# Scan decays of a hybrid encoder layer: bias in the exponential, feature decays by broadcast, time steps held by token

## The chip, the cores and the metric

One core of one Trainium2 chip runs the kernel. The metric is device microseconds of one execution; the profile adds one execution with the start and end of every instruction. A core has five instruction queues that run at the same time and meet only at semaphores: PE (TensorE, with its weight loads shown as PEld), DVE (VectorE), ACT (ScalarE), POOL (GpSimd) and SP (SyncE, which here only starts transfers). Each queue runs strictly in its own order: an instruction that waits holds up everything behind it on the same engine.

## The reference

One layer, sequence length 512, width 1024. The part that the change touches is the Mamba-2 style scan, forward and backward, 32 heads in 4 groups of 8, state 128, chunks of 128 tokens:

```
dt    = softplus(dt_in + dt_bias)                        # per token and head, two directions
a_cum = cumsum(dt * (-exp(a_log)))                       # inside each chunk
decay[l, s] = exp(a_cum[l] - a_cum[s]) where s <= l      # 0 elsewhere
y_diag = (C B^T * decay) @ (x * dt)
states = B^T @ (to_end * dt * x);  carried over the 4 chunks
y_off  = exp(a_cum) * (C @ carried_state)
y = y_fwd + y_bwd + d_skip * x;  then a gated group RMSNorm and three projections
```

Around it: RMSNorm, one wide input projection, a five-tap depthwise convolution with SiLU, windowed attention, gated merge, cross-attention over 256 memory rows, a SwiGLU FFN and a final RMSNorm.

## The kernel before, in words

Activations lie feature-major (features on partitions, 512 tokens along the row). Every projection step takes one weight block of 128x1024 (a `raw` tile, two buffers, loaded by SP), splits it into a high part `whi` (ACT, L128) and a low part `wlo` (DVE, or POOL for nine blocks, L129), and runs 24 matmuls (L138 to L140) into one of three PSUM banks `mm`. A list of steps is written out by the program; a scheduler then fixes the order of the instructions on each engine, and inserts the waits.

The steps that matter here, in order of time:

- **The time-step step** (`dt_step`, L338 to L398) runs once, at about 55 us, right after the first projection. It computes the softplus of the 64 rows (32 heads, two directions) with a polynomial on DVE, in tiles of 64 partitions by 512 tokens (L348 to L362), turns the results to token-major on PE (L368), forms running sums by matmuls with triangles (L380, L387, L391), and writes the sums `adr` to DRAM (L383), so that they can be read back broadcast over partitions. It leaves `nb` (log dt minus the running sum), `wt` and `dec`, token-major.
- **The convolutions** (`conv`, L403): ACT starts the tile `cvu` from PSUM (L408), DVE adds four taps (L411), ACT takes a tanh (L413), DVE finishes (L414). For the feature blocks `xs` PE then transposes the result (L467); that is placed in PE's queue one projection later.
- **The scan of a group** (`group_scan`): POOL weighs the tokens (`xw`, L492), PE forms the states (L500), DVE carries them (L505, L507). For each head, `head(h)`: SP loads two broadcast rows of `adr` into `rt` (128 partitions by 2x512, three buffers; L516); ACT takes the exponential of one half of its partitions into `ear` (L528; two buffers, one for a pair of heads); POOL writes a large negative number where the decay is zero, in place, for both directions (L530); then for each of the four chunks ACT takes an exponential with the bias `nb` in the forward direction (L536) and DVE adds `nb` in the backward direction (L538), after which one ACT exponential covers all four (L539). `both(h)` adds the two directions on POOL (`mt`, L545, frees `rt`), `times(h)` multiplies by C B^T on DVE (L550), `inner` and `arrive` are PE's products, and `gather` adds everything up; its last sum, on POOL (L585), frees `ear`.

The steps of a group's scan are interleaved with the projections and convolutions of the next group.

## Time and profile before

| | |
|---|---|
| runs | 1328.16, 1330.67, 1332.9 us, median 1330.67 |
| the profiled execution | 1331.93 us, span of its instructions 1330.2 us |
| busy over the span | PE 95%, PEld 76%, DVE 61%, ACT 44%, POOL 24% |
| 56 to 530 us | PE busy 430.88 of 474 us, DVE 375.47, ACT 237.53, POOL 201.64 |
| 530 to 1330 us | PE busy 786.53 of 800 us, DVE 400.74, ACT 308.62, POOL 99.51 |

A busy PE is one with a matmul in flight. The first stretch of the last two rows holds the time-step step, the convolutions and the scan; the second everything behind them. PEclk in the windows is the mean of the clock granted to TensorE, 1.00 for 2.4 GHz; its other level is half of that, 1.2 GHz.

### The profile page before, as it was taken

The numbers are of one execution on the slowest core, as the hardware profiler recorded it, in microseconds if no ns is written. First come the engines' busy times: TensorE is split into PE (matmuls) and PEld (weight loads), VectorE is DVE, ScalarE is ACT, GpSimd is POOL, SyncE is SP. The second block draws the span as 40 slices with busy tenths as digits, with TensorE's granted clock in tenths as the row PEclk, the third lists the DMA queues.
The fourth block names the chain that finished last, engine by engine and source line by source line (L and its number), as shares of the span: only waits on it lengthen the run. The fifth ranks groups of instructions, "written<-read, shape, count | busy, mean of one in ns | idle before, by whom it ended". The sixth has DMA issues, their size and how long they took to land.

```text
span 1330.2 us, 16362 instructions
## 1 busy us (share of the span) xinstructions
PE 1259.6 (95%) x6084; PEld 1016.9 (76%) x6084; DVE 811.2 (61%) x1359; ACT 579.1 (44%) x1001; POOL 316.4 (24%) x259
## 2 busy tenths in 40 slices
PE   6879998998999899999999999999999999999996
PEld 5667777786777687887667888888888888888886
DVE  5896788789678876678875334665443334442323
ACT  6437366266346434167865223444332223332220
POOL 3344263244354452321000002001121111110001
PEclk9999999999999899999999999999999999999998
DMA  6425344243233332321103333411232332223331
GB/s 241 141 97 151 123 151 127 60 131 116 82 103 111 95 96 90 113 88 64 49 33 111 98 98 106 143 64 52 92 96 97 102 102 95 96 91 103 88 99 64
DMA packets 45440, 134.95 MB, mean 101 GB/s; under 512 B 5104, under 2 KB 8560, under 8 KB 45360
## 3 DMA queue, kind: packets, MB, share of 16 engines
q1 hardware_dynamic: 43072, 129.77, 30.8%
q10 hardware_dynamic: 1584, 2.03, 0.5%
q0 software_dynamic: 704, 2.10, 0.4%
q8 instruction: 48, 0.79, 0.2%
q14 instruction: 32, 0.26, 0.1%
HBM read 129.55 MB, written 4.33 MB: 101 GB/s over the span
## 4 chain that ended last, share of the span: by engine, by line
PE 62%; DVE 12%; issue 10%; POOL 7%; ACT 5%; DMA 2%; SPq 0%; DVEq 0%; POOLq 0%; ACTq 0%
PE mm L138 18%; PE mm L139 18%; PE mm L140 18%; DVE rt L538 2%; DVE cvu L411 2%; DVE wlo L129 2%; POOL vv L585 1%; PE sb L815 1%; POOL mt L545 1%; ACT whi L128 1%; PE sb L802 1%; DMA rt<-adr 1%; POOL rsw L714 1%; POOL rt L530 1%; PE sb L988 1%
## 5 line engine op out<-in xcount | busy, mean ns | idle before, releaser
L128 ACT CAST whi<-raw 128x1024 fp32r<-128x1024 f32 (+2 forms) x192 | 198.9, 1037 | 451.9 <-PE mm L139 388.2
L138 PE MATMUL mm<-hh,whi 128*128 128x512 f32 x968 | 384.9, 398 | 6.9 <-DVE cvu L411 5.4
L139 PE MATMUL mm<-hl,whi 128*128 128x512 f32 x968 | 380.4, 393 | 1.8 <-DVE hl L310 1.8
L140 PE MATMUL mm<-hh,wlo 128*128 128x512 f32 x968 | 380.6, 393 | 1.1 <-DVE wlo L129 1.0
L129 DVE TENSOR_TENSOR wlo<-raw,whi 128x1024 fp32r<-128x1024 f32 (+2 forms) x193 | 242.4, 1257 | 128.4 <-ACT whi L128 122.4
L138 PEld LDWEIGHTS mm<-hh,whi 128*128 128x128 f32 x968 | 183.8, 190 | 46.3 <-issue 8.2
L140 PEld LDWEIGHTS mm<-hh,wlo 128*128 128x128 f32 x968 | 183.4, 189 | 41.3 <-DVE wlo L129 2.9
L139 PEld LDWEIGHTS mm<-hl,whi 128*128 128x128 f32 x968 | 183.6, 190 | 39.3 <-DVE hl L310 3.0
L185 POOL TENSOR_TENSOR sq_acc<-sq_acc,sq 128x512 f32<-128x512 f32 x14 | 24.8, 1771 | 264.4 <-ACT sq L184 264.4
L1041 POOL TENSOR_TENSOR fa<-fa,row 128x512 f32<-128x512 f32 x22 | 39.1, 1776 | 192.4 <-ACT fa L1040 192.4
L411 DVE SCALAR_TENSOR_TENSOR cvu<-mm,hcw,cvu 128x510 f32<-128x510 f32 (+1 forms) x96 | 70.9, 739 | 4.3 <-ACT cvu L408 3.9
L138 PE MATMUL mm<-vh,whi 128*128 128x512 f32 (+1 forms) x192 | 72.5, 378 | 0.0
L138 PE MATMUL mm<-fh,whi 128*128 128x512 f32 (+1 forms) x198 | 72.4, 366 | 0.0
L139 PE MATMUL mm<-fl,whi 128*128 128x512 f32 (+1 forms) x198 | 72.4, 365 | 0.0
L140 PE MATMUL mm<-fh,wlo 128*128 128x512 f32 (+1 forms) x198 | 72.4, 365 | 0.0
L140 PE MATMUL mm<-vh,wlo 128*128 128x512 f32 (+1 forms) x192 | 70.0, 364 | 0.0
L139 PE MATMUL mm<-vl,whi 128*128 128x512 f32 (+1 forms) x192 | 69.5, 362 | 0.0
L538 DVE TENSOR_SCALAR rt<-rt,nb 128x128 f32<-128x128 f32 x128 | 52.4, 465 | 21.3 <-POOL rt L530 19.6
L545 POOL TENSOR_TENSOR mt<-rt 128x512 f32<-128x512 f32 x32 | 47.7, 1493 | 72.1 <-ACT rt L539 34.1
L1043 DVE TENSOR_TENSOR ft<-fa,mm 128x512 f32<-128x512 f32 x22 | 15.1, 688 | 73.2 <-PE mm L140 71.0
L528 ACT ACTIVATE ear<-rt 64x1024 f32<-64x1024 f32 x32 | 33.9, 1059 | 56.6 <-POOL vv L585 51.9
L139 PE MATMUL mm<-ol,whi 128*128 128x512 f32 x128 | 50.0, 391 | 0.0
(234 smaller groups left out, 2061.4 us busy)
## 6 DMA issues: line engine op xcount, KB each, us to landing
raw<-in_w_in SPq DMA_DIRECT2D x69, 512.0 KB, 3.5
raw<-in_w_fi SPq DMA_DIRECT2D x44, 512.0 KB, 3.5
rt<-adr SPq DMA_DIRECT2D x64, 256.0 KB, 4.4
raw<-in_w_bs SPq DMA_DIRECT2D x16, 512.0 KB, 3.4
raw<-in_w_fo SPq DMA_DIRECT2D x16, 512.0 KB, 3.5
raw<-in_w_xk SPq DMA_DIRECT2D x8, 512.0 KB, 3.8
raw<-in_w_ba SPq DMA_DIRECT2D x8, 512.0 KB, 3.5
raw<-in_w_mo SPq DMA_DIRECT2D x8, 512.0 KB, 3.5
```

The source lines that it names most:

```text
L128: nc.scalar.copy(hi[:, t], raw[:, t])
L129: (nc.gpsimd if i in LO_POOL else nc.vector).tensor_tensor(lo[:, t], raw[:, t], hi[:, t].bitcast(F32), op=ALU.subtract)
L138: nc.tensor.matmul(acc, wh, xh[:, k0 + k], start=first and k == 0, stop=False)
L139: nc.tensor.matmul(acc, wh, xl[:, k0 + k], start=False, stop=False)
L140: nc.tensor.matmul(acc, wl, xh[:, k0 + k], start=False, stop=last and k == nk - 1)
L185: eng.tensor_tensor(acc, acc, sq, op=ALU.add)
L411: nc.vector.scalar_tensor_tensor(u[:, b], acc[:, a], w5[j], u[:, b], op0=ALU.mult, op1=ALU.add)
L528: nc.scalar.activation(st["ear", h // 2][own], rt[own], AF.Exp)
L538: nc.vector.tensor_scalar(r, r, st["nb"][:, c, e0:e0 + 1], None, op0=ALU.add)
L545: nc.gpsimd.tensor_tensor(mt, st["rt", g, h][:, 0], st["rt", g, h][:, 1], op=ALU.add)
L1041: nc.gpsimd.tensor_tensor(a, a, st["row2"], op=ALU.mult)
L1043: nc.vector.tensor_tensor(t, a, st["fp", 2 * j + 1], op=ALU.mult)
```

## The change

Five edits; no arithmetic of the layer is left out.

1. **Time steps by token.** The projected rows are turned to token-major first (four PE transposes), and the whole softplus runs on tiles of 128 partitions by 256. The polynomial's multiply and add, two instructions before, become one `scalar_tensor_tensor`. The log is taken later. The turns of the results fall away (12 transposes and three ACT copies).
2. **`a_log` comes broadcast** over the partitions, 64 columns instead of one, from the host.
3. **Bias in the exponential, backward too.** DVE's add of `nb` and the one 512-wide exponential give way to four 128-wide exponentials with a bias: 4 DVE and 1 ACT instruction less, 4 ACT more, for each of 32 heads.
4. **Feature decays by broadcast.** The exponential of the running sums is taken once, on 64 rows by 512, and written to DRAM (`edr`); `ear` is then loaded by two transfers for each pair of heads (64 partitions each, 256 KB each, on SP's queue) instead of by ACT. The third and later loads of a group are issued behind the gather that frees their buffer.
5. **One transfer for `rt`** instead of two: 512 KB for both directions.

```diff
-        nc.scalar.activation(v, acc[0:64], AF.Identity, bias=vec[0:64, V_DTB:V_DTB + 1])
-        nc.scalar.activation(e, v, AF.Abs)
+        def slot(i):
+            return x1[:, i // 2, 256 * (i % 2):256 * (i % 2) + 256].rearrange("p (c e) -> p c e", c=NCH)
+        v, e, den, s2, pl, dta, ld, acm = (slot(i) for i in range(8))
+        raw, rows, erows = (x1[0:64, i] for i in (5, 6, 7))
+        nc.scalar.activation(raw, acc[0:64], AF.Identity, bias=vec[0:64, V_DTB:V_DTB + 1])
+        for c in range(NCH):
+            nc.tensor.transpose(tpv[:, c], raw[:, c * P:(c + 1) * P], ident[0:64, 0:64])
+        nc.scalar.activation(an, vec[:, V_AL:V_AL + 64], AF.Exp)
+        nc.scalar.activation(e, tpv, AF.Abs)
+        nc.vector.tensor_copy(v, tpv)
...
-        for n in (13, 11, 9, 7, 5, 3, 1):
-            nc.vector.tensor_tensor(pl, pl, s2, op=ALU.mult)
-            nc.vector.tensor_scalar(pl, pl, 2.0 / n, None, op0=ALU.add)
-        nc.vector.tensor_tensor(pl, pl, e, op=ALU.mult)
+        for n in (15, 13, 11, 9, 7, 5, 3):
+            nc.vector.scalar_tensor_tensor(pl, pl, 2.0 / n, s2, op0=ALU.add, op1=ALU.mult)
+        nc.vector.scalar_tensor_tensor(pl, pl, 2.0, e, op0=ALU.add, op1=ALU.mult)
...
-        dat = tok(dta, t256(5, 0))
-        dtt = tok(dt, t256(5, 1))
-        ldt = tok(ld, t256(7, 1))
...
+        nc.vector.tensor_copy(rows, fm[0:64])
+        nc.sync.dma_start(adr, rows)
+        nc.scalar.activation(erows, rows, AF.Exp)
+        nc.sync.dma_start(edr, erows)
...
-            for d in range(2):
-                nc.sync.dma_start(rt[:, d], adr[32 * d + e0:32 * d + e0 + 1, :].broadcast_to([P, S]))
+            nc.sync.dma_start(rt, adr.rearrange("(d e) s -> e d s", d=2)[e0:e0 + 1].broadcast_to([P, 2, S]))
+        def earows(i):
+            def f():
+                st["ear", i] = ear = st["sp"].tile([P, 2, S], F32, tag="ear", name="ear", bufs=2)
+                for k in range(2):
+                    e0 = 8 * g + 2 * i + k
+                    nc.sync.dma_start(ear[64 * k:64 * k + 64], edr.rearrange("(d e) s -> e d s", d=2)[e0:e0 + 1]
+                                      .broadcast_to([64, 2, S]))
+            return f
...
-                nc.scalar.activation(st["ear", h // 2][own], rt[own], AF.Exp)
...
-                for c in range(NCH):
-                    r, e0 = rt[:, 0, c * P:(c + 1) * P], 8 * g + h
-                    nc.scalar.activation(r, r, AF.Exp, bias=st["nb"][:, c, e0:e0 + 1])
-                    r, e0 = rt[:, 1, c * P:(c + 1) * P], e0 + 32
-                    nc.vector.tensor_scalar(r, r, st["nb"][:, c, e0:e0 + 1], None, op0=ALU.add)
-                nc.scalar.activation(rt[:, 1], rt[:, 1], AF.Exp)
+                for d in range(2):
+                    for c in range(NCH):
+                        r, e0 = rt[:, d, c * P:(c + 1) * P], 32 * d + 8 * g + h
+                        nc.scalar.activation(r, r, AF.Exp, bias=st["nb"][:, c, e0:e0 + 1])
...
             if t >= LAG3 + GLAG and (t - LAG3 - GLAG) % 2 == 0:
-                order.append(ga[(t - LAG3 - GLAG) // 2])
+                i = (t - LAG3 - GLAG) // 2
+                order += [ga[i]] + el[i + 2:i + 3]
+            if t in EL:
+                order.append(el[EL.index(t)])
```

The order on the engines at three places. On PE, the time-step step's products before (`x_69` is the tile `x1`, which this step uses as scratch space; the projection that is under way has the rows `mm<-hh`):

```order
L140 MATMUL mm<-hh,wlo 128x512
L368 MATMUL sb<-cst,x_69 128x64 x4
L380 MATMUL sa<-tri,x_69 32x128 x8
L387 MATMUL sb<-x_69,tri 128x4x32 x2
L391 MATMUL sb<-x_69,cst 128x256
```

and now:

```order
L142 MATMUL mm<-vh,wlo 128x256
L376 MATMUL sa<-tri,x_69 32x128 x8
L381 MATMUL sb<-x_69,tri 128x4x32 x2
L385 MATMUL sb<-x_69,cst 128x256
L427 MATMUL sb<-cst,bf 128x128 x4
```

The running sums stood at row 312 of PE's queue, behind the third feature block's projection; they stand at row 224 now, in the middle of the second memory-key projection (`vh`), 51 matmuls of a 512-wide and 36 of a 256-wide projection earlier.

On DVE, behind the time-step step, where the first heads begin, before:

```order
L395 TENSOR_TENSOR nb<-x_69 128x256
L396 TENSOR_TENSOR wt<-sb,x_69 128x256
L414 SCALAR_TENSOR_TENSOR xs<-cvt,cvu 128x512
L398 TENSOR_TENSOR wt<-wt,x_69 128x256
L538 TENSOR_SCALAR rt<-rt,nb 128x128
L129 TENSOR_TENSOR wlo<-raw,whi 128x1024
L411 SCALAR_TENSOR_TENSOR cvu<-mm,hcw,cvu 128x510
L538 TENSOR_SCALAR rt<-rt,nb 128x128
L411 SCALAR_TENSOR_TENSOR cvu<-mm,hcw,cvu 128x511
```

and now:

```order
L369 SCALAR_TENSOR_TENSOR x_69<-x_69,an 128x256
L370 TENSOR_SCALAR x_69<-x_69 128x256
L412 SCALAR_TENSOR_TENSOR cf<-cvt,cvu 128x512
L409 SCALAR_TENSOR_TENSOR cvu<-mm,hcw,cvu 128x510
L386 COPY x_69<-sa 64x512
L409 SCALAR_TENSOR_TENSOR cvu<-mm,hcw,cvu 128x511 x2
L392 TENSOR_TENSOR wt<-sb,x_69 128x256
L396 TENSOR_TENSOR nb<-x_69 128x256
L409 SCALAR_TENSOR_TENSOR cvu<-mm,hcw,cvu 128x510
L394 TENSOR_TENSOR wt<-wt,x_69 128x256
```

No head has an instruction on DVE between the convolutions' taps any more, and the step's last product (`x_69,an`) stands ahead of the second convolution's end (`cf`) where it stood behind two feature blocks.

On SP, in the scan of the first group, before:

```order
L516 DMA rt<-adr 128x512 x4
L120 DMA raw<-in_w_in 128x1024 x3
L516 DMA rt<-adr 128x512 x2
L120 DMA raw<-in_w_bs 128x1024
```

and now:

```order
L513 DMA rt<-adr 128x2x512 x3
L122 DMA raw<-in_w_in 128x1024
L522 DMA ear<-edr 64x2x512 x2
L513 DMA rt<-adr 128x2x512
L122 DMA raw<-in_w_in 128x1024
L513 DMA rt<-adr 128x2x512
L122 DMA raw<-in_w_bs 128x1024
L522 DMA ear<-edr 64x2x512 x2
L122 DMA raw<-in_w_in 128x1024
```

The weight loads now stand behind loads of `ear` as well as of `rt`.

## Rows read from the trace of the kernel before

**Rows 1.** Waits of PE, 56 to 530 us: total, times, longest
```profile
PE sb L467 <- DVE xs L414: 19.9, 6, 5.7
PE mm L138 <- DVE cvu L411: 5.4, 3, 2.2
...
PE sb L368 <- DVE x L361: 4.2, 1, 4.2
PE sa L560 <- DVE mt L550: 2.9, 1, 2.9
```

**Rows 2.** Timeline of PE: start, us, instruction, idle time before it
```profile
225.06 0.63 PE L467 MATMUL sb<-cst,xs 128*128 128x128 f32 x4 [4.16 <-DVE xs L414]
...
333.11 1.09 PE L467 MATMUL sb<-cst,xs 128*128 128x128 f32 x4 [5.70 <-DVE xs L414]
...
445.08 1.09 PE L467 MATMUL sb<-cst,xs 128*128 128x128 f32 x4 [4.22 <-DVE xs L414]
```

**Rows 3.** Windows: busy us of PE, PEld, DVE, ACT, POOL; PEclk, DMA share, GB/s
```profile
90.00:146.00 56.00, 47.06 (x232) 36.44 (x231) 42.78 (x63) 33.10 (x58) 22.28 (x20) 0.94 0.45 129
190.00:230.00 40.00, 33.09 (x154) 26.94 (x153) 35.25 (x57) 25.57 (x46) 18.17 (x16) 0.91 0.43 136
330.00:340.00 10.00, 6.89 (x22) 5.65 (x23) 6.59 (x11) 4.49 (x7) 2.11 (x2) 0.66 0.65 192
440.00:460.00 20.00, 15.11 (x51) 9.72 (x50) 17.68 (x28) 6.45 (x11) 10.56 (x9) 0.83 0.44 131
```

**Rows 4.** Windows of line L538 alone: busy us of DVE (x), clock, transfers
```profile
211.00:225.00 14.00, 5.73 (x12) 1.00 0.51 150
322.00:333.00 11.00, 3.71 (x8) 0.93 0.60 177
430.00:444.00 14.00, 4.80 (x12) 1.00 0.42 123
```

**Rows 5.** Groups by line: busy us, mean ns, idle before and releaser
```profile
L538 DVE TENSOR_SCALAR rt<-rt,nb 128x128 f32<-128x128 f32 x128 | 52.4, 465 | 21.3 <-POOL rt L530 19.6 <-DMA raw<-in_w_in 1.7
...
L536 ACT ACTIVATE rt<-rt,nb 128x128 f32<-128x128 f32 x128 | 41.0, 391 | 0.5 <-POOL rt L530 0.2
...
L528 ACT ACTIVATE ear<-rt 64x1024 f32<-64x1024 f32 x32 | 33.9, 1059 | 56.6 <-POOL vv L585 51.9 <-DMA rt<-adr 4.2
...
L539 ACT ACTIVATE rt<-rt 128x512 f32<-128x512 f32 x32 | 19.9, 627 | 12.8 <-DVE rt L538 12.8
```

**Rows 6.** Timeline of DVE in the time-step step
```profile
57.02 0.75 DVE L411 SCALAR_TENSOR_TENSOR cvu<-mm,hcw,cvu 128x510 f32<-128x510 f32 x1 [3.63 <-ACT cvu L408]
...
58.68 3.33 DVE L349 RECIPROCAL x<-x 64x512 f32<-64x512 f32 x1
...
67.66 0.68 DVE L354 TENSOR_TENSOR x<-x 64x512 f32<-64x512 f32 x1
...
78.16 2.88 DVE L354 TENSOR_TENSOR x<-x 64x512 f32<-64x512 f32 x1
...
102.91 0.43 DVE L395 TENSOR_TENSOR nb<-x 128x256 f32<-128x256 f32 x1
```

**Rows 7.** Timeline of POOL in the same step
```profile
77.79 2.71 POOL L129 TENSOR_TENSOR wlo<-raw,whi 128x1024 fp32r<-128x1024 f32 x1 [2.69 <-ACT whi L128]
```

**Rows 8.** Timeline of PE: starts of the first feature and the second key projection
```profile
66.01 0.47 PE L138 MATMUL mm<-hh,whi 128*128 128x512 f32 x1 [1.64 <-DVE cvu L411]
...
71.57 0.28 PE L138 MATMUL mm<-vh,whi 128*128 128x256 f32 x1
```

**Rows 9.** Waits of PE, 108 to 180 us
```profile
PE sb L500 <- POOL xw L492: 2.6, 2, 1.7
PE sb L500 <- DVE hin L507: 1.6, 1, 1.6
```

**Rows 10.** Timeline of POOL at the first head
```profile
112.06 1.23 POOL L530 TENSOR_SCALAR_AFFINE_SELECT rt<-rt 128x512 f32<-128x512 f32 x2 [11.73 <-ACT ear L528]
```

**Rows 11.** Waits of ACT, 100 to 530 us
```profile
ACT whi L128 <- DMA raw<-in_w_in: 8.8, 4, 3.3
```

More of the change, by code (lines that the diff above doesn't have):

```diff
@@ L63 @@
 RAWB, WB = 2, 3
+EL = (2, 4)
 def weave(a, b):
@@ L91, in bidir_hybrid_layer @@
     adr = dram.tile([64, S], F32, tag="adr", name="adr")
+    edr = dram.tile([64, S], F32, tag="edr", name="edr")
     def bank(tag):
@@ L339, in dt_step @@
         acc = proj(w, st["hh"], st["hl"])
-        v, e, den, s2, pl = (x1[0:64, i] for i in range(5))
-        def t256(i, o):
-            return x1[:, i, 256 * o:256 * o + 256].rearrange("p (c e) -> p c e", c=NCH)
-        nc.scalar.activation(v, acc[0:64], AF.Identity, bias=vec[0:64, V_DTB:V_DTB + 1])
-        nc.scalar.activation(e, v, AF.Abs)
+        def slot(i):
[3 more added lines that the diff above has]
+        nc.scalar.activation(raw, acc[0:64], AF.Identity, bias=vec[0:64, V_DTB:V_DTB + 1])
+        tp = bank("sb")
+        tpv = tp[:, 0:256].rearrange("p (c e) -> p c e", c=NCH)
+        for c in range(NCH):
+            nc.tensor.transpose(tpv[:, c], raw[:, c * P:(c + 1) * P], ident[0:64, 0:64])
+        an = st["sp"].tile([P, 64], F32, tag="an", name="an")
+        nc.scalar.activation(an, vec[:, V_AL:V_AL + 64], AF.Exp)
+        nc.scalar.activation(e, tpv, AF.Abs)
+        nc.vector.tensor_copy(v, tpv)
         nc.scalar.activation(e, e, AF.Exp, scale=-1.0)
@@ L379, in dt_step @@
             for c in range(NCH):
-                nc.tensor.matmul(fm[32 * d:32 * d + 32, c * P:(c + 1) * P], dat[:, c, 32 * d:32 * d + 32],
+                nc.tensor.matmul(fm[32 * d:32 * d + 32, c * P:(c + 1) * P], dta[:, c, 32 * d:32 * d + 32],
                                  tri[d], start=True, stop=True)
-        nc.scalar.copy(x1[0:64, 6], fm[0:64])
-        nc.sync.dma_start(adr, x1[0:64, 6])
         tm = bank("sb")
@@ L386, in dt_step @@
         for d in range(2):
-            nc.tensor.matmul(tv[:, :, 32 * d:32 * d + 32], tri[d], dat[:, :, 32 * d:32 * d + 32],
+            nc.tensor.matmul(tv[:, :, 32 * d:32 * d + 32], tri[d], dta[:, :, 32 * d:32 * d + 32],
                              start=True, stop=True)
@@ L390, in dt_step @@
         ov = tot[:, 0:256].rearrange("p (c e) -> p c e", c=NCH)
-        nc.tensor.matmul(ov, ones, dat, start=True, stop=True)
-        acm = t256(4, 0)
+        nc.tensor.matmul(ov, ones, dta, start=True, stop=True)
+        nc.vector.tensor_copy(rows, fm[0:64])
+        nc.sync.dma_start(adr, rows)
+        nc.scalar.activation(erows, rows, AF.Exp)
+        nc.sync.dma_start(edr, erows)
         nc.scalar.copy(acm, tv)
         nc.scalar.activation(dec, ov, AF.Exp)
-        nc.vector.tensor_tensor(nb, ldt, acm, op=ALU.subtract)
         nc.vector.tensor_tensor(wt, ov, acm, op=ALU.subtract)
         nc.scalar.activation(wt, wt, AF.Exp)
-        nc.vector.tensor_tensor(wt, wt, dtt, op=ALU.mult)
+        nc.vector.tensor_tensor(wt, wt, dt, op=ALU.mult)
+        nc.scalar.activation(ld, ld, AF.Ln)
+        nc.vector.tensor_tensor(nb, ld, acm, op=ALU.subtract)
         dump("dt", dt)
@@ L605, in group_scan @@
         hd, bo, ti = ([w(h) for h in range(HPG)] for w in (head, both, times))
-        nn, ar, ga, gs = ([w(i) for i in range(4)] for w in (inner, arrive, gather, gate))
+        nn, ar, ga, gs, el = ([w(i) for i in range(4)] for w in (inner, arrive, gather, gate, earows))
         order = []
@@ L1186, in layout @@
     vecs[32:64, V_DTB] = a["dt_bias_bwd"][0]
-    vecs[0:32, V_AL] = a["a_log_fwd"][0]
-    vecs[32:64, V_AL] = a["a_log_bwd"][0]
+    vecs[:, V_AL:V_AL + 32] = a["a_log_fwd"][0][None]
+    vecs[:, V_AL + 32:V_AL + 64] = a["a_log_bwd"][0][None]
     vecs[:, V_DSK:V_DSK + 16] = _cols(np.repeat(a["d_skip"][0], 64))
```

24 lines of the change are left out of this document (6 added, 18 removed).

## The prediction

> **What bounds the kernel now.** I read the waits of TensorE first, since it is nearly always the busy engine and its gaps are what a change elsewhere can win. In the stretch with the time-step step and the scan, the reader is to see that almost all of PE's idle time is put down to DVE [rows 1]: 19.9 us in six waits for a finished convolution block (`xs`, L414, wanted by the transposes L467), 5.4 us for a PSUM bank that a convolution's taps hold (L411), 4.2 us for the time-step step's result (L361), 2.9 us for a head's product (L550). Behind 530 us PE has next to no gap, so nothing of the change can count there.
>
> The timeline of PE shows that three of the six waits make most of it: 4.16, 5.70 and 4.22 us, 14.1 together, near the end of groups 0, 1 and 2 [rows 2]. The windows add what a wait costs behind it: after such a gap the granted clock falls to its lower level, 1.2 GHz, for a while. A window's loss is its width times what is missing from 1.00 [rows 3]: 3.4 us in 90 to 146 (two falls, 1.7 each, one behind the wait for L361 and one behind POOL's `xw`), 3.6 in 190 to 230 (two), 3.4 in 330 to 340, 3.4 in 440 to 460. So a gap of 4 or 5 us costs 6 to 9. DVE is busy for 35.25 of 40 and 17.68 of 20 us there, ACT for 25.57 and 6.45 [rows 3]: DVE is the late one.
>
> **The change, part by part.** *The adds of `nb` leave DVE.* 128 instructions, 52.4 us [rows 5]. What counts is how much of them lies in the queue ahead of a late `xs`. Line L538 alone has 5.73, 3.71 and 4.80 us of DVE in the 11 to 14 us that end at the three waits [rows 4]. Without them `xs` comes that much earlier, as long as nothing else is late: min(4.16, 5.73) + min(5.70, 3.71) + min(4.22, 4.80) = 12.1 us of the 14.1. The falls of the clock behind these three should go with them: 1.8 (one of the two in 190 to 230) + 3.4 + 3.4 = 8.6. I take **-20.7** for both. Bounds: nothing, if another link of the convolution's chain is as late; 22.7 if all of it goes.
>
> The other three waits for `xs` (19.9 - 14.1 = 5.8), the 2.9 for `mt` and the other fall in 190 to 230 (1.8) have DVE's backlog as their cause too, but I did not trace L538 into each of them. I take a third of the 10.5: **-3.5**; bounds 0 and -10.5.
>
> *ACT.* It loses the 32 exponentials into `ear`, 33.9 us, and 32 of 512 columns, 19.9 us, and gains 128 of 128 columns, at 391 ns at most 50.0 us [rows 5]: 3.8 us less. More is worth that ACT stood still for 51.9 us in front of `ear`, waiting for POOL's last sum of two pairs earlier (L585) to free the buffer [rows 5], with weight splits and tanhs queued behind it; and that POOL's masking of a head no longer waits for ACT to have read it. That gain I book nowhere; it is what makes the -20.7 likely, since ACT's tanh is the link in front of `xs`.
>
> *The time-step step.* The waits ahead of the running sums are 5.4 + 4.2 = 9.6 us, with one fall of the clock, 1.7. What will remain? DVE: its first instruction will be a copy of some 0.4 us, so the reciprocal starts at 58.68 + 0.4 = 59.1 [rows 6]. From there to `dta`, in the new order, stand: the reciprocal on half the columns (at most 3.33, I take half, 1.7), 12 instructions of two operands on 128x256 (0.43 each, L395: 5.2), one scalar one (0.4), six taps (0.75: 4.5), one 128x256 product (0.4) and one 0.68 [rows 6], in all 12.9: ready at 72.0. PE: it began the second key projection at 71.57, of which 1.64 was a wait that the shorter chain should remove [rows 8]; with half of that projection (a quarter of the 5.56 us that the 512-wide one before it took, 1.4) and the four new transposes (some 0.4, an estimate) it reaches the sums at 71.7.
>
> But the same instruction took 0.68 us at one time and 2.88 at another [rows 6], and in the second case POOL was in the middle of a `wlo` from 77.79 to 80.50 [rows 7]: DVE's product began at 78.16, ended 81.04, 0.5 after POOL. POOL's two-operand instructions and DVE's exclude each other, and such a meeting costs 2.2 us. The new chain still has 12 of them, with POOL's `wlo` beside it; at one `wlo` per weight block of 5.56 us some three fall into the 13 us, and I let two be met: 4.4 us, `dta` at 76.4, a wait of 4.7 at PE in place of 9.6, the clock's fall kept. **-4.9.** Bounds: no meeting, -11.0 (9.3 and 1.7); each of the 12 met, 26 us, a wait of 27, +17. The Trainium skill, GPSIMD Engine Reference, section Key points, says that GpSimd shares its SBUF interfaces with VectorE and contends with instructions of two SBUF inputs or in a two-port mode. By that rule the fused polynomial is no lighter for contention than the old one, since each fused instruction has two SBUF inputs; taken for every instruction it gives the +17. The trace agrees with it for the 2.88; the 0.68 of the same instruction shows that not each meets one, and the sum goes by the rows.
>
> *The first heads come earlier.* POOL waited 11.73 us before the first head, at 112.06 [rows 10]. `dta` 18 us earlier moves that to some 90 to 95, into a stretch where POOL has only `wlo` to do. Group 0 then weighs its tokens on time: of the waits for `xw` and the carry, 2.6 + 1.6 = 4.2 [rows 9], I keep one of 1.3 (the mean of the two), and the second fall of 90 to 146 (1.7) goes: **-4.6**; bounds 0 and -5.9.
>
> *What is added in waits.* The exponentials now stand where DVE's adds stood, behind POOL's masks; DVE waited 19.6 us there [rows 5]. ACT inherits these waits, with weight splits behind it. DVE's cost PE only in part; I take a third: **+6**; bounds 0 and 19.6. The `ear` transfers move 8.4 MB more (32 of 256 KB) on SP's queue, behind buffers and ahead of weights; their cover is that only 4 of the weight splits waited for a load, 8.8 us [rows 11]. I cost them at nothing here; without that cover they are the rival below. The two new writes and loads of tables lie beside PE's projections, and `vecs` is 32 KB longer at the start, a sixteenth of a weight block.
>
> **Sum.** -20.7 - 3.5 - 4.9 - 4.6 + 6 = -27.7. The profiled execution took 1331.93, 1.3 above the median of the runs, 1330.67; so 1303 as a median.
>
> **Rivals.** *The next link is as late* (the tanh behind the exponentials on ACT, POOL's masks, the splits). Half of the 20.7 comes, nothing of the 3.5, and the added waits are 12: -10.4 - 4.9 - 4.6 + 12 = -7.9, 1323. For it: queues are fixed, and a gap that closes shows the next; DVE stays the busiest helper. Against it: ACT loses work and its longest waits too.
>
> *DVE's relief reaches no `xs` at all*: only the time-step step and the first heads remain, -9.5 + 6 = -3.5, 1327, about no change. Against it: L538 stands between the taps in the very stretches that end late [rows 4].
>
> *More comes*: every wait listed goes and nothing is added, -11.0 - 5.9 - 22.7 - 10.5 = -50.1, 1281.
>
> *Slower: SP's queue.* An `ear` load waits on SP for the same release (L585) for which ACT waited 51.9 us in 14 waits [rows 5], and the weights stand behind it. If all of that comes through to PE, -33.7 + 51.9 = +18, 1349. It decides from some 65% of these waits on (33.7 of 51.9). For it: the new order has weight loads directly behind `ear`. Against it: weights lie ready before their split in all but four cases [rows 11], with two raw and three split buffers; a wait of up to 5.56 us, one projection, should pass unseen. The Trainium skill, DMA: Bandwidth & Descriptors, section on queues, rings and completion order, adds that descriptors are consumed in ring order on each DMA engine, so that weights also stand behind the bytes of `ear`; no row here separates the two.
>
> **Chances.** The forecast (1290 to 1315) 0.55; next link late (1315 to 1325) 0.18; more comes (below 1290) 0.10; no relief 0.07; slower 0.10. A measurement here tells a change of some 0.3%, 4 us, from none. Faster 0.83, the same 0.07, slower 0.10. The range reaches half into the two neighbours of the forecast: 1284 to 1323, which leaves 0.2 out.
>
> **What would show it.** Right: no wait of PE over 2 us for L412 (the new `xs`) near the end of groups 0 to 2, PEclk 1.00 there, POOL's first mask before 96 us, one wait of some 5 us ahead of the running sums. Wrong: waits of PE for weights (`whi`, `wlo`), SP's waits at `ear` over 6 us, or ACT waiting at its exponentials for POOL's masks by more than 20 us in all. The time-step step would prove me wrong by a wait over 10 us at L376.

## The result and the profile after

The changed kernel takes 1317.43 us (median of 4 runs, 1316.42 to 1317.72) against 1330.82 of the kernel before in the same session: a ratio of 0.9899, 95% interval 0.9884 to 0.9914, or 13.4 us less. Forecast were 27.7 less. The time lies inside the range and the sign is right, but the gain is a little less than half of what was forecast.

TensorE's waits in the changed kernel, to be held against [rows 1] (total, times, longest):

```profile
PE sb L465 <- DVE xs L412: 20.3, 5, 8.5
PE sa L376 <- DVE x L369: 5.1, 1, 5.1
PE sb L498 <- POOL xw L490: 2.6, 5, 0.9
...
PE mm L140 <- DVE cvu L409: 0.9, 1, 0.9
```

The waits for a PSUM bank (5.4 before, 0.9 now) and for a head's product (2.9, now gone) have left. The waits for `xs`, on which three quarters of the forecast gain rested, are as long as before: 20.3 against 19.9 us, the longest 8.5 against 5.7. The clock tells the same (windows around the waits: width, busy us of PE, PEld, DVE, ACT, POOL, then PEclk, transfers):

```profile
70.00:110.00 40.00, 32.12 (x168) 27.17 (x167) 29.61 (x39) 25.14 (x54) 21.77 (x20) 0.87 0.59 168
185.00:215.00 30.00, 24.24 (x121) 19.54 (x120) 23.86 (x33) 21.80 (x55) 12.60 (x14) 0.94 0.57 170
290.00:305.00 15.00, 11.65 (x52) 9.04 (x51) 11.64 (x16) 10.06 (x24) 7.42 (x7) 0.77 0.52 177
395.00:415.00 20.00, 11.53 (x54) 8.97 (x53) 16.20 (x21) 10.86 (x26) 10.50 (x9) 0.74 0.54 156
```

Width times what is missing from 1.00 gives 5.2, 1.8, 3.5 and 5.2, together 15.7 us, where the windows of [rows 3] gave 13.8: none of the clock's loss is gone. DVE still has 16.2 us of work in the last window of 20, but ACT and POOL, which have some 11 there, now stand for long. What they wait for shows in their own waits (ACT, POOL and SP's queue, 56 to 530 us; the last line is of the kernel before):

```profile
ACT rt L539 <- POOL rt L532: 76.8, 19, 10.1
POOL rt L532 <- DMA rt<-adr: 52.1, 17, 7.5
SPq L522 <- POOL vv L585: 58.0, 12, 9.4
SPq L522 <- POOL rt L532: 15.0, 2, 7.5
SPq L513 <- POOL mt L545: 48.9, 22, 6.6
...
SPq L516 <- POOL mt L545: 113.8, 27, 13.8
```

ACT stands 76.8 us at its exponentials for POOL's masks; before it stood 51.9 us in front of `ear` [rows 5]. POOL in turn stands 52.1 us for the row loads, which it did not wait for before. SP stands 58.0 + 15.0 + 48.9 = 121.9 us for buffers, hardly more than the 113.8 of before; 73.0 of it now at the loads of `ear`. The last late `xs` shows the line of waits (POOL, ACT and PE; start, us, instruction, idle time before it):

```profile
401.10 1.23 POOL L532 TENSOR_SCALAR_AFFINE_SELECT rt<-rt 128x512 f32<-128x512 f32 x2 [3.52 <-DMA rt<-adr]
...
401.77 0.98 ACT L539 ACTIVATE rt<-rt,nb 128x128 f32<-128x128 f32 x3 [5.97 <-POOL rt L532]
402.66 1.03 ACT L130 CAST whi<-raw 128x1024 fp32r<-128x1024 f32 x1
403.59 0.62 ACT L411 ACTIVATE cvt<-cvu 128x512 f32<-128x512 f32 x1
...
406.04 1.12 PE L465 MATMUL sb<-cst,xs 128*128 128x128 f32 x4 [8.47 <-DVE xs L412]
```

The tanh of the convolution (L411) stands behind three exponentials that wait for a mask that waits for a row; PE stands 8.47 us at the end of it.

### The profile page after: what moved, and what is told of

The parts are those of the page before. It is cut to its first block, busy times and chain, and to the rows that moved or that the text cites. A ratio compares the mean times of both kernels' runs of the same rounds, so it can differ in the third digit from the quotient of the medians.

```text
span 1314.7 us, 16234 instructions
## 1 busy us (share of the span) xinstructions
PE 1254.8 (95%) x6076; PEld 1014.5 (77%) x6076; DVE 774.7 (59%) x1226; ACT 564.2 (43%) x1062; POOL 322.1 (25%) x259
## 4 chain that ended last, share of the span: by engine, by line
PE 66%; issue 6%; POOL 4%; DVE 4%; ACT 2%; DMA 2%; SPq 0%; DVEq 0%; POOLq 0%; ACTq 0%
PE mm L140 19%; PE mm L141 19%; PE mm L142 19%; DMA rt<-adr 2%; PE sb L818 1%; PE sb L805 1%; DVE wlo L131 1%; PE sb L991 1%; PE sa L960 1%; POOL rsw L717 1%; PE sa L560 1%; POOL mt L545 1%; POOL xw L490 1%; PE sb L498 1%; DVE cvu L409 1%
## 5 line engine op out<-in xcount | busy, mean ns | idle before, releaser
L539 ACT ACTIVATE rt<-rt,nb 128x128 f32<-128x128 f32 x256 | 79.5, 390 | 76.9 <-POOL rt L532 76.8
L532 POOL TENSOR_SCALAR_AFFINE_SELECT rt<-rt 128x512 f32<-128x512 f32 x64 | 53.7, 862 | 53.0 <-DMA rt<-adr 52.1
```

Of the source, the lines that this page charges most:

```text
L532: nc.gpsimd.affine_select(out=rt[:, d].rearrange("p (c l) -> p c l", c=NCH), in_=rt[:, d].rearrange("p (c l) -> p c l", c=NCH), pattern=[[ ...
L539: nc.scalar.activation(r, r, AF.Exp, bias=st["nb"][:, c, e0:e0 + 1])
```

## The experiments

All ratios are to the kernel before on the same chip; "gain" is one minus the ratio, times 1330.8 us. The difference of two gains is known to some 3 to 4 us (the halves of the two 95% intervals, added in quadrature). Letters of theories hold within a series. The change falls into four parts, and most kernels below are sums of them: **T**, the time-step step by token; **X**, the eight biased exponentials in place of VectorE's additions; **L**, the feature decays loaded from DRAM instead of ACT's exponential; **R**, one row load of 512 KB instead of two of 256.

| parts | ratio (95%) | gain, us |
|---|---|---|
| T | 0.9937 (0.9915 to 0.9959) | 8.4 |
| X L R | 0.9952 (0.9933 to 0.9971) | 6.4 |
| T L R | 1.0009 (0.9996 to 1.0022) | -1.2 |
| T X L | 0.9868 (0.9849 to 0.9888) | 17.6 |
| T X R | 0.9813 (0.9792 to 0.9835) | 24.9 |
| T X | 0.9810 (0.9790 to 0.9829) | 25.3 |
| T X L R, the change | 0.9899 (0.9884 to 0.9914) | 13.4 |

**First series.** *T alone*: `head` and the loads as before the change, `dt_step` as changed but for the two lines that feed L.

```
-        nc.scalar.activation(erows, rows, AF.Exp)
-        nc.sync.dma_start(edr, erows)
```

> Edits 1 and 2 alone: the time-step step by token, the heads as before. Theory A (the gain of the heads was lost to ACT, which now stands at its exponentials until POOL's masks are through, and those wait for the load of rt): this part gives the 4 us that the trace of the changed kernel shows of it, 1327 (1323 to 1329), with PE waiting some 5 us for the running sums. Rival B (the step was sized rightly, and the loss is all in the scan): 1321, the -9.5 of the prediction. Rival C (the earlier first heads collide with the convolutions): 1331 or more.

1322.19 us, where rival B had it, and not theory A. PE's wait at the running sums is 5.1 us, and the `xs` waits stay as they were (21.1 us, seven, longest 5.7). T gives what it was to give.

*X, L and R without T*: the old `dt_step`, with one exponential and one write for the loads of L.

```
+        nc.scalar.activation(x1[0:64, 3], x1[0:64, 6], AF.Exp)
+        nc.sync.dma_start(edr, x1[0:64, 3])
```

> Edits 3 to 5 alone, with the old time-step step (and the one exponential and write for the broadcast feature decays). Theory A: the heads give some 9 us, 1322 (1318 to 1326), and ACT still waits over 60 us for POOL's masks in the scan (76.8 in the changed kernel). Rival C (the heads' gain is eaten only because the first heads now collide with the convolutions of group 0): 1310 or less.

1324.55 us; `xs` waits 17.6 us, ACT's waits for the masks 76.0. The heads' part is the one that falls short.

*R undone*:

```
-            nc.sync.dma_start(rt, adr.rearrange("(d e) s -> e d s", d=2)[e0:e0 + 1].broadcast_to([P, 2, S]))
+            for d in range(2):
+                nc.sync.dma_start(rt[:, d], adr[32 * d + e0:32 * d + e0 + 1, :].broadcast_to([P, S]))
```

> The changed kernel with rt loaded by two transfers of 256 KB again (edit 5 undone). Theory A, in the form that the length of the one load is what makes the masks late (5.7 us to landing, 4.4 before): the forward mask can start when the first half is there, POOL's 52.1 us of waits for rt fall below 35, and the time falls by 2 to 6 us, to 1311 to 1315. Rival D (the load is issued late, since SP stands at other loads; its length does not matter): within 2 us of 1317.

1313.13 us, as theory A had it. POOL's longest wait for a row falls from 7.5 to 3.5 us, but the total only to 46.0 instead of below 35, and the `xs` waits stay (20.9).

*L's loads issued by POOL instead of SP*, in `earows`:

```
-                    nc.sync.dma_start(ear[64 * k:64 * k + 64], edr.rearrange("(d e) s -> e d s", d=2)[e0:e0 + 1]
+                    nc.gpsimd.dma_start(ear[64 * k:64 * k + 64], edr.rearrange("(d e) s -> e d s", d=2)[e0:e0 + 1]
```

> The changed kernel with the loads of ear issued from POOL's queue, where the sum that frees their buffer runs, so that SP never waits for it (58.0 us of SP's waits in the changed kernel). Theory D (rt is late because SP stands at ear): POOL's waits for rt fall from 52.1 us to below 30, ACT's for the masks from 76.8 to below 50, time 1305 to 1312, less some for 32 issues of about 0.5 us on POOL. Theory A with the length of the load as the cause: SP's waits vanish and the time stays within 3 us of 1317.

1324.19 us, ratio 0.9947 (0.9927 to 0.9967). SP no longer stands at `ear`, but rows are as late (POOL's waits 58.7 us) and the `xs` waits grow to 26.0. The wait now stands in POOL's queue, which also makes the sums that free the row buffers, so this run does not clear SP; the fifth series comes back to it.

**Second series.** *Four row buffers*, the memory taken from one of the two `ear` buffers, and a *control* with the one `ear` buffer alone:

```
-RB = 3
+RB = 4
...
-                st["ear", i] = ear = st["sp"].tile([P, 2, S], F32, tag="ear", name="ear", bufs=2)
+                st["ear", i] = ear = st["sp"].tile([P, 2, S], F32, tag="ear", name="ear", bufs=1)
...
-                order += [ga[i]] + el[i + 2:i + 3]
+                order += [ga[i]] + el[i + 1:i + 2]
```

> The changed kernel with four row buffers instead of three; the memory for the fourth comes from one ear buffer instead of two (its load is issued behind the gather that frees it, which is where SP stood before). Theory A (the ring: a row buffer is freed by POOL's sum, then loaded, then masked, then exponentiated, and ACT stands in line at its exponentials with the tanh of the convolutions behind them): POOL's waits for the row loads fall from 52 us to under 20, ACT's waits for POOL's masks from 77 to under 45, PE's waits for xs from 20.3 to under 12, time 1303 to 1311. Theory B (the eight exponentials by themselves, 25 us more of ACT work in the groups, are what holds up the tanh): POOL's waits may fall, ACT's groups stay as they are in front of the tanh, PE's waits for xs stay 18 to 22, time 1315 to 1319.

> Control for the four row buffers: the changed kernel with one ear buffer instead of two and still three row buffers. Both theories: 1315 to 1320, PE's waits for xs 18 to 23; SP's waits at ear are no longer than 58 us in all. A time above 1322 would mean that the one buffer itself costs something, and the run with four row buffers is then read against this one.

1312.02 and 1312.46 us, ratios 0.9859 (0.9845 to 0.9874) and 0.9858 (0.9843 to 0.9874). Neither time is one that was expected, but they agree: the fourth buffer gives nothing, and rows are waited for 55.4 us with it and 58.5 without. Both gain 5 us on the change; in the profiled executions 2.2 to 2.5 of it lie ahead of the time-step step, which no edit touches (last section).

*X undone* (VectorE adds `nb` backward, one exponential over four chunks):

```
-                for d in range(2):
...
+                    nc.vector.tensor_scalar(r, r, st["nb"][:, c, e0:e0 + 1], None, op0=ALU.add)
+                nc.scalar.activation(rt[:, 1], rt[:, 1], AF.Exp)
```

> The changed kernel with one part undone: the backward rows get their bias from VectorE again (four additions of 128 columns) and one exponential of 512 columns instead of four of 128. Theory A (ACT stands for the masks, whatever number of exponentials is behind them): ACT's waits stay between 65 and 90 us, PE's waits for xs 18 to 24, time 1314 to 1321. Theory B (the number of exponentials): ACT loses 32 times about 0.85 us, PE's waits for xs fall under 14, time 1306 to 1312. The prediction's own reason (the additions on VectorE made xs late): time 1325 or more.

1331.23 us: nothing is left of the gain, and the `xs` waits are 32.5 us. That the additions on VectorE made `xs` late was right, and they are worth 14.6 us here. But T, L and R together are 9.6 us slower than T alone: one of the two edits that got no cost, L and R, costs.

*The sum of the directions on VectorE*, in `both`:

```
-                nc.gpsimd.tensor_tensor(mt, st["rt", g, h][:, 0], st["rt", g, h][:, 1], op=ALU.add)
+                nc.vector.tensor_tensor(mt, st["rt", g, h][:, 0], st["rt", g, h][:, 1], op=ALU.add)
```

> The changed kernel with the sum of the two directions on VectorE instead of POOL, so that a row buffer no longer waits for POOL's queue to be free. Theory A (the ring through POOL): SP's waits for the sum fall from 49 us to under 20, POOL's for the row loads from 52 to under 25, PE's waits for xs under 14, time 1304 to 1312. Theory B: ACT has the same work in the same order, 1315 to 1319. Against A: the sums now stand in VectorE's queue ahead of its convolutions, and where they wait for ACT's exponentials the multiplications that give xs wait too: time 1318 to 1326, and PE's waits for xs over 22.

1309.23 us, ratio 0.9845 (0.9828 to 0.9862). Rows are waited for even longer (111.9 us, POOL having less else to do), ACT's waits are 70.3; the `xs` waits become ten short ones, the longest 3.7. A gain, but not by the row loads.

**Third series.** *L undone*, *L and R undone*, and the latter with the sum on VectorE:

```
+                if h % 2 == 0:
+                    st["ear", h // 2] = st["sp"].tile([P, 2, S], F32, tag="ear", name="ear", bufs=2)
+                own = slice(64 * (h % 2), 64 * (h % 2) + 64)
+                nc.scalar.activation(st["ear", h // 2][own], rt[own], AF.Exp)
...
-                order += [ga[i]] + el[i + 2:i + 3]
-            if t in EL:
-                order.append(el[EL.index(t)])
+                order += [ga[i]]
```

> The changed kernel with one part undone: the decays of the features come from one more exponential on ACT (64x1024, as before the change) instead of being loaded from DRAM. Theory C (the two edits that the prediction costed at nothing, the loads of the feature decays and the single 512 KB row load, cost 9 us together, the time by which the run with the additions back on VectorE, 1331.2, stands over the run with the time-step edits alone, 1322.2; 4.3 of it is the single load, by the run with two row loads): 1310 to 1314.5, and POOL's longest wait for a row load under 7.5 us. Theory D (those 9 us are spread over other causes, such as the phase of the clock): 1316 to 1319. Theory B (ACT's work is what holds up the tanh): 32 more exponentials of about 0.9 us, 1320 to 1326.

> The changed kernel without its two DMA edits: feature decays by ACT's exponential and two row loads of 256 KB as before the change; the time-step edits and the eight biased exponentials stay. If the parts add up (theory C): the time-step edits alone gave 1322.2, the removal of VectorE's additions gives 13.8 more (1331.2 against 1317.4), 1306 to 1311. Theory D: 1312 to 1318. Theory B: ACT carries the most work of all versions, 1318 or more.

> The version before this one with the sum of the two directions on VectorE instead of POOL. The sum on VectorE gave 8 us on the changed kernel, of which 3.4 us is an early clock fall that has nothing to do with it: 1301 to 1306 if it adds to the removal of the DMA edits; 1308 or more if both act on the same wait (the row load that comes late because POOL frees its buffer late).

1305.93, 1305.92 and 1294.04 us; the first and the last are faster than any theory had them. The last has a ratio of 0.9714 (0.9697 to 0.9732), 38.1 us less than before, the best of all. L costs 11.5 us beside R and 7.7 without it; R costs 0.4 by itself, which is nothing, and 4.2 beside L. In the version without L (waits of PE and ACT, then two of the windows shown above for the change):

```profile
PE sb L463 <- DVE xs L410: 7.5, 7, 2.5
PE sa L562 <- DVE mt L552: 5.5, 2, 3.4
PE sa L376 <- DVE x L369: 5.1, 1, 5.1
```

```profile
ACT ear L532 <- POOL vv L587: 32.8, 9, 8.2
...
ACT rt L541 <- POOL rt L534: 4.2, 5, 1.7
```

```profile
290.00:305.00 15.00, 15.00 (x70) 12.40 (x69) 13.57 (x17) 13.05 (x28) 9.66 (x10) 1.00 0.37 122
395.00:415.00 20.00, 20.00 (x98) 16.80 (x97) 17.31 (x21) 16.30 (x32) 11.19 (x10) 1.00 0.40 123
```

This is the profile that was forecast for the change: no `xs` wait above 2.5 us, and a clock of 1.00 at the ends of the groups. ACT stands 32.8 + 4.2 = 37.0 us for the gather and the masks, not 76.8; POOL has no wait for rows among its larger ones. How the heads stand in POOL's program can be read off its timeline, first in the change, then without L, each with the load of a row by SP:

```profile
259.00 1.23 POOL L532 TENSOR_SCALAR_AFFINE_SELECT rt<-rt 128x512 f32<-128x512 f32 x2 [3.23 <-DMA rt<-adr]
260.19 1.02 POOL L585 TENSOR_TENSOR vv<-vv,ear 128x384 f32<-128x384 f32 x1
261.61 1.41 POOL L532 TENSOR_SCALAR_AFFINE_SELECT rt<-rt 128x512 f32<-128x512 f32 x2 [0.40 <-DMA rt<-adr]
266.30 3.52 POOL L545 TENSOR_TENSOR mt<-rt 128x512 f32<-128x512 f32 x2 [3.28 <-PE sa L560]
274.87 1.57 POOL L532 TENSOR_SCALAR_AFFINE_SELECT rt<-rt 128x512 f32<-128x512 f32 x2 [5.06 <-DMA rt<-adr]
276.42 1.02 POOL L585 TENSOR_TENSOR vv<-vv,ear 128x384 f32<-128x384 f32 x1
...
269.09 0.43 SPq L513 DMA_DIRECT2D rt<-adr  x1
```

```profile
256.21 1.29 POOL L547 TENSOR_TENSOR mt<-rt 128x512 f32<-128x512 f32 x1 [1.23 <-issue]
259.42 1.28 POOL L547 TENSOR_TENSOR mt<-rt 128x512 f32<-128x512 f32 x1 [1.92 <-PE sa L562]
269.23 1.03 POOL L587 TENSOR_TENSOR vv<-vv,ear 128x384 f32<-128x384 f32 x1 [8.53 <-DVE ear L586]
271.43 3.22 POOL L534 TENSOR_SCALAR_AFFINE_SELECT rt<-rt 128x512 f32<-128x512 f32 x4 [1.17 <-ACT ear L532]
...
257.53 3.58 SPq L511 DMA_DIRECT2D rt<-adr  x2
```

Without L, ACT's exponential into `ear` waits for the gather (`vv`) to free the buffer, and the masks wait for that exponential. So the four masks of a pair stand behind the gather, and the row that a sum (`mt`) has made room for is issued 15.9 us before its mask (257.53 to 273.4, the third of the four masks). In the change the heads are not held back in this way: masks stand ahead of the gather, the row is issued 5.8 us before its mask (269.09 to 274.87), and a row of 512 KB took 5.7 us to land (median; 5.5 without L). The gather queues behind the masks that wait.

The two traces show the same for all 32 heads. Without L the first mask of a head always starts 1 us or more behind the landing of its row, in the median 15.4 us. In the change 23 of the 32 start within 0.3 us of it. SP is seldom to blame: of the 29 rows that need a buffer back, 24 were issued within 0.7 us of the end of the sum that freed it, and some 41 of the 52 us that POOL waits lie in front of these. So the rows are late because the masks follow close behind the sums, and not because SP issues them late or they take longer.

**Fourth series.** *L's loads two time slots later in the code*:

```
-EL = (2, 4)
+EL = (4, 6, 8, 10)
...
-                order += [ga[i]] + el[i + 2:i + 3]
+                order += [ga[i]]
```

> The changed kernel with the same loads of the feature decays, each issued two time slots later in SP's program (the first two at slots 4 and 6 instead of 2 and 4, the last two two slots behind the gather that frees their buffer instead of right behind it), still two slots ahead of their use. Theory E (SP's queue: SP stands at these loads for POOL to free the buffer, and the row loads and weight loads queued behind them are issued late): SP's waits at ear fall from 73 us to under 25, POOL's waits for the row loads from 52 to under 25, ACT's for the masks from 77 to under 40, PE's for xs from 20.3 to under 12, time 1304 to 1310, near the 1305.9 of the version without these loads. Theory F (the traffic itself, 32 loads of 256 KB beside the others, or a changed order on POOL and ACT, not SP's standing): SP's waits at ear may fall, POOL's waits for the rows stay over 40 us, time 1314 to 1320.

1314.35 us, ratio 0.9881 (0.9862 to 0.9900). The scheduler put the loads almost where they had been, and SP stood 73.7 us at them as before: the edit did not do what it should, and the run tells nothing.

**Fifth series.** *SP's standing without the traffic*: L undone, and loads of 64x8 into a small tile at L's places, freed by a POOL addition behind the gather.

```
+                st["tk", i] = tk = st["sp"].tile([P, 8], F32, tag="tk", name="tk", bufs=2)
+                for k in range(2):
+                    nc.sync.dma_start(tk[64 * k:64 * k + 64], adr[8 * g + 2 * i + k:8 * g + 2 * i + k + 1, 0:8]
+                                      .broadcast_to([64, 8]))
...
+                nc.gpsimd.tensor_tensor(st["tk", i][:, 0:1], st["tk", i][:, 1:2], vv[:, 0:1], op=ALU.add)
```

> The version with the feature decays by ACT's exponential (1305.9), with SP made to stand as in the changed kernel: at the places of the loads of the feature decays SP issues loads of 64x8 instead, into a small tile that POOL frees by one more addition of one column behind its gather. Theory E (SP's standing): SP's waits at these loads 40 us or more, POOL's waits for the row loads over 30 us, time 1314 to 1320. Theories F (traffic) and G (the heads held back by the exponential): POOL's waits for the rows under 15 us, 1303 to 1309. Under 25 us of waits at the small loads the run tells nothing about E.

1312.35 us, ratio 0.9862 (0.9840 to 0.9884). SP stands 70.6 us, and yet the rows are in time: ACT waits 5.4 us for the masks. The time lies above the 1305.93 without L, and between both expectations; the control of the next series says how much of that is the addition.

*The heads held back by an exponential of one column*, the change otherwise as it is:

```
+                nc.scalar.activation(st["ear", h // 2][own, 0, 0:1], rt[own, 0, 0:1], AF.Exp)
```

> The changed kernel with its loads of the feature decays, and ahead of each head's masks one exponential of 64x1 on ACT that reads the row and writes the first column of the feature decays (the value that the load has brought), so that a pair of heads is again held back until POOL's gather has freed the buffer and the loads have landed; the loads are issued at the first head of each pair. Theory G (the heads were held back by the old exponential and now run ahead of their row loads): ACT's waits for POOL's masks fall from 77 to under 25 us, POOL's for the row loads from 52 to under 25, time 1303 to 1311. Theories E and F (SP stands and the traffic is there as before): POOL's waits for the rows stay over 40 us, time 1315 or more, and the heads that now also wait for the landing of the feature decays can make it 1320 or more.

1351.24 us, ratio 1.0144 (1.0126 to 1.0163). The column reads one direction alone; the other direction's masks still ran ahead, heads were torn into halves, and ACT stood 113.8 us. It holds back half a head and so does not test its theory.

**Sixth series.** *Both directions held back*, as the old exponential did, and a *control*: L undone, with POOL's additional addition (and a memset for it), without the small loads.

```
+                    st["tk", h // 2] = st["sp"].tile([P, 2], F32, tag="tk", name="tk", bufs=2)
+                own = slice(64 * (h % 2), 64 * (h % 2) + 64)
+                nc.scalar.activation(st["tk", h // 2][own], rt[own, :, 0], AF.Exp)
...
+                nc.gpsimd.tensor_tensor(st["tk", i][:, 0:1], st["tk", i][:, 1:2], vv[:, 0:1], op=ALU.add)
```

> The changed kernel, its loads of the feature decays as they are, and ahead of each head's masks one exponential of 64x2 on ACT that reads both directions of the row and writes a small tile, which POOL frees by an addition of one column behind its gather: a pair of heads is held back as the old exponential held it, and nothing waits for the landing of the feature decays. In POOL's program the four masks of a pair now stand behind the gather and ahead of the two sums, as in the version without the loads. Theory G (the heads ran ahead of their row loads): ACT's waits for POOL's masks fall from 77 to under 20 us, POOL's for the row loads from 52 to under 15, PE's for xs from 20.3 to under 12, time 1304 to 1312. Theory F (the traffic of the loads): POOL's waits for the rows over 35 us, time 1315 or more.

> Control: the version with the feature decays by ACT's exponential (1305.9) with POOL's addition of one column behind each gather and a memset ahead of it, no small loads. If the 6 us that the version with the small loads took more were due to POOL's additional work or another order of the programs: 1309 to 1314. If they were due to SP's standing: 1304 to 1308.

The control takes 1310.69 us, ratio 0.9852 (0.9837 to 0.9867). So of the 6.4 us by which the standing SP was slower than the version without L, 4.8 belong to POOL's addition and its memset and 1.7 to the standing, by the medians; the 1.7 is less than such a difference can tell from nothing. The kernel with the heads held back takes 1320.98, ratio 0.9927 (0.9913 to 0.9941), and its ACT:

```profile
ACT tk L534 <- POOL tk L590: 62.2, 14, 8.5
...
ACT rt L543 <- POOL rt L536: 11.9, 14, 2.4
```

The rows are in time now, and ACT stands as long as in the change, for the gather: 62.2 + 11.9 in place of 76.8. So theory G, as far as it forecast the time, failed: 1304 to 1312 was expected. POOL's addition, the bytes of the loads and SP's standing would explain some 10 of the 15 us over the version without L (4.8 + 4.0 + 1.7 by the medians, the 4.0 from the next series); the rest is open. That rows come late is how the wait shows in the change; to bring them in time did not mend it.

**Seventh series.** *The traffic alone*, on the version without L: two stores of each `xs` tile to DRAM, the programs of the four computing engines in the scan unchanged; and *the change without the traffic*: the loads bring 8 of 512 columns, and one of them is used for all (the output is no longer the layer's), with TensorE's program unchanged and the others nearly so (some 30 of ACT's 470 rows and 16 of VectorE's 450 stand elsewhere).

```
+                [nc.sync.dma_start(scr[(8 * g + 2 * i + k) % 4], xs) for k in range(2)]
```

```
-                                      .broadcast_to([64, 2, S]))
+                                      .broadcast_to([64, 2, 8]))
...
+                    nc.vector.tensor_tensor(ear[:, d, P:S], ear[:, d, 0:1].broadcast_to([P, S - P]), st["yo", i, d][:, t], op=ALU.mult)
```

> The version with the feature decays by ACT's exponential (1305.9) and, as 8 MB of traffic, two stores of each xs tile to DRAM (32 of 256 KB, as many bytes as the loads of the feature decays), issued by SP; the programs of TensorE, VectorE, ACT and POOL stay row for row as they were in the scan. Theory F (traffic): 1313 to 1320, and the median landing of the row loads over 5.5 us. Theory G (the order of the programs): 1304 to 1309.

> The changed kernel with loads of 64x2x8 in place of 64x2x512: the loads are there and SP stands for POOL as before, but only one column of the feature decays is brought, and it is used for all columns (so part of the computation is changed). TensorE's program is the same row for row. Theory F (traffic): 1304 to 1310, and POOL's waits for the row loads under 25 us. Theory G (order of the programs): 1314 to 1320, and POOL's waits for the rows over 35 us.

1309.96 us, ratio 0.9843 (0.9828 to 0.9857), and 1315.13, ratio 0.9883 (0.9867 to 0.9900). The first lies between both expectations, and its rows land in 5.5 us (median) as without the stores. Without its 8 MB the change gains 2.2 us, and its rows are waited for as before:

```profile
POOL rt L532 <- DMA rt<-adr: 54.5, 21, 6.3
```

With 8 MB the other version loses 4.0 us. So the bytes are 2 to 4 us of the 11.5, by differences that are themselves known to 3 or 4. With the 1.7 of SP's standing that is half at most by the medians, and could be more within their errors. What is left is put down to the order of the programs because no other cause was found, not because a run has shown it.

## Why the prediction was wrong, and what of it held

**T held.** Forecast for the time-step step and the first heads: 4.9 + 4.6 = 9.5 us; measured alone 8.4. The wait at the running sums was to be 4.7 and is 5.1, PE arriving at 73.6 (forecast 71.7) and `dta` being ready at 78.7 (76.4). The meetings of DVE with POOL's splits were to be two, at 2.2 us each. DVE and POOL of the changed kernel:

```profile
63.55 2.15 DVE L360 TENSOR_TENSOR x<-x 128x256 f32<-128x256 f32 x1
...
67.75 3.96 DVE L364 SCALAR_TENSOR_TENSOR x<-x 128x256 f32<-128x256 f32 x4
...
72.28 0.41 DVE L364 SCALAR_TENSOR_TENSOR x<-x 128x256 f32<-128x256 f32 x1
...
73.28 2.53 DVE L364 SCALAR_TENSOR_TENSOR x<-x 128x256 f32<-128x256 f32 x1
```

```profile
63.03 2.39 POOL L131 TENSOR_TENSOR wlo<-raw,whi 128x1024 fp32r<-128x1024 f32 x1 [2.44 <-ACT whi L130]
...
68.12 2.38 POOL L131 TENSOR_TENSOR wlo<-raw,whi 128x1024 fp32r<-128x1024 f32 x1 [0.23 <-ACT whi L130]
73.18 2.35 POOL L131 TENSOR_TENSOR wlo<-raw,whi 128x1024 fp32r<-128x1024 f32 x1 [2.68 <-ACT whi L130]
```

At the 0.41 us of the row at 72.28, the others (one, four and one instructions) should take 0.41, 1.64 and 0.41; they took 1.7, 2.3 and 2.1 more, each overlapping a `wlo` and ending 0.3 to 1.2 us behind it. Three meetings, 6.1 us in place of the 4.4 that were allowed for. The whole chain from the reciprocal to `dta` still took 17.4 us against a forecast of 17.3 (12.9 + 4.4), since the rest of it was 1.6 us shorter: two errors cancelled, which is luck. `dta` was late because the chain began at 61.32 and not at 59.1. The first mask starts at 90.07 (forecast 90 to 95), and PE waits 0.3 us for `xw` in 108 to 180.

**X held, as a sum of terms.** -20.7 - 3.5 + 6 = -18.2 was forecast. On top of T, without L and R, X gives 16.9. The additions were a cause of the late `xs`: without L these waits fall from 21.1 us (T alone) to 7.9, and with L they are back at 20.9. The version with T and X alone stands at 25.3 us of gain beside the 27.7 forecast. One reason that the prediction gave was not needed for it: ACT still stands 34.2 us in front of `ear` there, for the gather.

**The step that failed is the one that costed the `ear` transfers at nothing** ("their cover is that only 4 of the weight splits waited for a load"), and with it the sentence before the time-step step that called it a gain that ACT would no longer stand in front of `ear` and the masks no longer behind it. L costs 11.5 us, known to some 3.5. The slower rival named the right part of the change, but not the way: it had weights late behind SP. They are not (ACT's splits waited 10.1 us for weights in four waits, 8.8 in four before), SP stands 121.9 us in all where it stood 113.8, and SP's standing by itself cost 1.7 us. The traffic is 2 to 4 us, not the bulk of it. The Trainium skill, DMA: Bandwidth & Descriptors, section on queues, rings and completion order, was cited for weights that stand behind the bytes of `ear`; the run with 8 columns in place of 512 gained 2.2 us more, which is less than such a difference can tell from nothing.

What the runs show in its place: the exponential that L takes away had held back the heads of a pair until the gather of two pairs earlier was through. Without it the masks stand earlier in POOL's program than their rows can be there (23 of 32 start within 0.3 us of their row's landing, none in the version without L), ACT stands 76.8 us instead of 37.0 with the tanh behind it, and the `xs` waits that X removes come back by another way, 20.3 us. So far the traces show it. That this lost hold is what costs the time is argued and not shown. For it: the bytes and SP's standing, each measured by itself, leave half of the 11.5 us or more by their medians. Against it: two columns of the exponential, put back, restored the order of POOL's masks and brought the rows in time, yet the kernel took 1320.98 us, as ACT then stood for the gather, and a fourth row buffer gave nothing either. Which row of the programs costs the time stays open. A kernel with the change's loads and, row for row, the programs of the version without them was not built, since the scheduler sets the order anew with each edit.

The test written ahead, "ACT waiting at its exponentials for POOL's masks by more than 20 us in all", came true with 76.8, and so did the one on SP (waits at `ear` over 6 us: 73.0 in all, 9.4 the longest). The term behind the first, +6 as a third of 19.6, fits neither case: without L that wait is only 3.8 to 4.2 us, and with L a third of it would be 25.6.

## What to carry to other kernels

An instruction that waits may also keep later work from running ahead of its data; before a wait is removed, ask what will stand at the head of that engine's queue instead, and what stands behind it. Cost each edit of a change by itself, also the ones that only move work from a busy engine to the transfers: here one of them took 11.5 of 25 us. And where a scheduler sets the order, read the new order at the place that is late. Here most rows were issued as promptly as in the version without L and landed in 5.7 us against 5.5, and yet POOL stood 52.1 us for them, since its masks had moved up.

## What was not expected of the hardware

The first 56 us are the same work in all these kernels, and yet the granted clock there differs from one profiled execution to the other (the change, then the version with one `ear` buffer; windows, with PEclk third from the end; below each, where VectorE begins the time-step step):

```profile
0.00:56.00 56.00, 42.67 (x166) 31.83 (x167) 35.00 (x54) 32.17 (x54) 14.65 (x19) 0.94 0.60 205
...
61.32 1.74 DVE L359 RECIPROCAL x<-x 128x256 f32<-128x256 f32 x1
```

```profile
0.00:56.00 56.00, 41.84 (x181) 31.17 (x182) 35.33 (x55) 34.56 (x57) 16.50 (x19) 1.00 0.62 205
...
59.16 1.74 DVE L359 RECIPROCAL x<-x 128x256 f32<-128x256 f32 x1
```

0.94 against 1.00 is 3.4 us of 56 at a wait of 2.6 us ahead of L155 that both have: in one the clock falls to 1.2 GHz there, in the other it stays at 2.4. At the time-step step 2.2 us of it are left. These are single executions. The mean clock of the change's own four executions goes from 0.982 to 0.986, so the fall may belong to the execution and not to the kernel; no run here tells which. A difference of 2 or 3 us between two versions is therefore read as an edit's only after the early stretch has been looked at. Between the change (0.94) and the version without L (0.94) it is not at work. The change without its bytes had 0.97 there and began the step at 59.43, 1.9 us earlier than the change, so that its gain of 2.2 need not be the bytes'. The control with POOL's addition had 1.00 and began it 1.5 us earlier than the version without L, and was slower all the same.

One addition of one column on POOL behind each gather, with a memset, cost 4.8 us (1310.69 against 1305.93), although POOL is busy for less than half of that stretch and the other engines' programs in the scan stayed nearly row for row as they were. The addition itself takes 0.19 us (median). ACT does not wait for it: the gather ahead of it releases `ear`, and ACT's waits for that are 35.2 us against 32.8. VectorE's next instruction on `vv` waits for it, 10.4 us in nine waits, against 8.2 in nine for the gather without it. Why it costs 4.8 us is open.
